# A two-layer decoder trunk: gated linear attention staggered against the projections around it

## The chip, the cores and the metric

The program runs on one core of a Trainium2 chip. Its time is the device time of one execution in microseconds (us); lower is better. The engines are TensorE (PE: matrix products and transposes, with the weight loads listed as PEld), VectorE (DVE), ScalarE (ACT), GpSimd (POOL) and SyncE (SP, which issues most loads). PE's products accumulate in eight PSUM banks of 512 float32 columns each.

## The reference, cut to what matters

Two layers work on 512 tokens of 1024 channels. Each layer normalizes, projects with one wide input matrix, runs three mixers side by side, adds their output projection, and then runs a feed-forward block. The change touches one mixer, the gated linear attention (4 heads, key width 32, value width 64), and the places of two projections around it:

```python
def reference(x, ...):
    for l in range(DEPTH):                                   # 2
        h = rmsnorm(x, attn_norm[l])
        (q, kc, vc, ksl, vsl, kwn, vwn, gts, gq, gk, gv, ga, gr, uv) = split_columns(h @ w_in[l])
        o_nsa = nsa_mixer(q, kc, vc, ksl, vsl, kwn, vwn, gts, ...)
        o_gla = gla_mixer(gq, gk, gv, ga, gr, gla_w_up[l], gla_b_up[l], gla_norm[l])
        o_sg = spatial_gating(uv, ...)
        x = x + jnp.concatenate([o_nsa, o_gla, o_sg], axis=-1) @ w_out[l]
        h = rmsnorm(x, ffn_norm[l])
        x = x + (jax.nn.silu(h @ w_gate[l]) * (h @ w_up[l])) @ w_down[l]
    return rmsnorm(x, final_norm)

def gla_mixer(q, k, v, a_lr, r, w_up, b_up, norm_g):
    g = log_sigmoid(a_lr @ w_up + b_up) / 16                 # (S, 4 heads, 32)
    ...
    def step(state, inp):                                    # one chunk of tokens
        bcum = jnp.cumsum(gc, axis=2)
        o_inter = jnp.einsum('bhck,bhkv->bhcv', qc * jnp.exp(bcum), state)
        decay = exp(where(causal, bcum[i] - bcum[j], -inf))  # per key channel
        attn = jnp.einsum('bhik,bhjk,bhijk->bhij', qc, kc, decay)
        o_intra = jnp.einsum('bhij,bhjv->bhiv', attn, vc)
        state = exp(blast) * state + einsum(kc * exp(blast - bcum), vc)
        return state, o_inter + o_intra
    ...
    return rmsnorm(o, norm_g) * silu(r)
```

## The kernel before, in words

**Projections.** The tokens are four tiles of 128. Every float32 operand of a projection is split into a high and a low part, and `mm3` (L327 to L329) makes one product out of three: high by high, high by low, low by high. `w_rows` (L315) loads a block of weights from SP's queue into a `raw` buffer (three of them); `w_split` (L305) makes the high part on ACT (L309) and the low part on DVE (L312) in an `hl` buffer (four of them). `proj_tok` multiplies a token tile at a time: 8 blocks of 128 channels by three products are 24 matmuls for a tile and 96 for a projection. The projections that matter here are gr (the gate r, 256 columns), B (keys and values of two branches of the sparse attention, 512 columns) and q (512 columns); `ev_gr`, `ev_b` and `ev_q` evacuate a tile's bank. `c1` is a small projection ahead of them, whose evacuation `ev_c1` also transposes a little tile `ga`.

**PSUM.** `psum(tag)` hands out banks by turns: g is banks 0 and 1 (projections), t is 2 and 3, s is 4 to 6, o is 7. The linear attention also names its banks directly.

**The linear attention.** The chunk of this kernel is a token tile, 128 wide, so there are four steps t = 0 to 3 with a state carried between them. A causal 128x128 block is cut into the diagonal and seven levels (squares of side 64, 32, ... 1), so that each square's decay splits into a factor for its queries and one for its keys. One step is a chain over engines:

1. Logits (L814, L815): a 0/1 matrix `tsel` times the split log gates gives sums of log gates for nine sets of 128 columns. They go through bank 6 in three groups of 512, 512 and 128 columns, and ACT takes each group's exp into `E` (L816).
2. Factors on DVE: seven products with the queries (L824, tile `xq`), two multiplies of `E` by the keys (L825, called xk in the code), and a fill of the diagonal of `at` by `diag` (L828).
3. Level products on PE (L834): 7 levels by 4 heads, 32 rows and 64 columns each, into banks 2 to 5.
4. Picks on DVE (L841): seven masked copies of the banks into `at`.
5. Outputs into bank 7: from the second step on, `xi` (queries by decay, on DVE) times the carried state `sbd`, a 128x256 matrix that is zero outside its four head blocks (L846), and `at` times the values for each head (L848). ACT copies the bank to `osb`.
6. Carry, not in the last step: a transpose of decayed keys (L853), a copy on ACT, the product with all values, 128x256 (L857), in bank 6, and on DVE the mask `bdm` and the update of `sbd` (L859, or L862 and L863).

**The order.** In the program's text gr stands before the four steps and B behind them. Engines run their own queues in order, but the order in each queue is made by a tile scheduler from the text and priorities: splits of weights are moved forward by 400 (`WPRI`), evacuations by 600 (`EPRI`). So in the queues as built, gr's matmuls stand ahead of the chain, and B's are laced through it. `tsel` is loaded at the start of a layer's mixer from ACT's queue into float32 and rounded by POOL to the type that PE wants (L791, L793). `diag` comes from the product of queries and keys, `qk`, made on POOL (L795) and summed by PE over each head (L798). Behind B come the key preparation `prep_k` (its transposes are L915), then q, then the sparse attention.

## Time and profile before

| what | value |
|---|---|
| median of 3 runs | 1318.18 us (1316.72 to 1322.44) |
| the profiled execution | 1317.21 us, of which the span 1315.4 us |
| PE busy | 97% of the span |
| DVE busy | 72% |
| ACT busy | 50% |
| POOL busy | 13% |
| DMA | 150.48 MB, 114 GB/s over the span |

The profile is one execution. Its span runs from the first to the last instruction, and the rows below give times in us from the span's start. A busy PE is not PE at its peak: the chip grants TensorE a clock that has two levels, 2.4 and 1.2 GHz, listed as a share (1.00 and 0.50), and a matmul is counted busy at either. The linear attention of layer 0 lies at about 94 to 160 us, that of layer 1 at about 737 to 806 us.

### The profile page before, as it was taken

What the parts mean: (1) busy time and instruction counts of PE and PEld (TensorE: products, weight loads), DVE (VectorE), ACT (ScalarE), POOL (GpSimd) and SP (SyncE); (2) the same over time, 40 slices, a digit from 0 to 9 for tenths busy, and PEclk for the clock granted to TensorE, in tenths of its full rate; (3) what the DMA queues carried; (4) which work ended last, traced back from release to release, by engine and by line L of the source; (5) the groups of instructions that cost most, each with busy time, mean ns of one, the idle gap of its engine ahead of it and who ended that gap; (6) DMA issues with size and microseconds to landing.
All of it is one profiled execution on the core that took longest, in us unless ns stands there. A gap on an engine that the chain in (4) does not pass through costs nothing.

```text
span 1315.4 us, 17968 instructions
## 1 busy us (share of the span) xinstructions
PE 1278.4 (97%) x6688; PEld 1045.4 (79%) x6688; DVE 944.5 (72%) x1637; ACT 658.5 (50%) x1200; POOL 174.0 (13%) x156
## 2 busy tenths in 40 slices
PE   8899999999999999999999999999999999999997
PEld 6788777778888888888888877677888888888786
DVE  5756889977855675577646578999777458736775
ACT  6663347865532543354446523678644435515532
POOL 2111121113000100010302102111210001000102
PEclk9998999999999999999999989999999999999999
DMA  7551221015334885483346302200533448754731
GB/s 234 143 162 40 65 64 33 17 64 145 96 101 123 208 229 141 108 200 107 110 104 168 105 9 64 81 17 17 137 103 96 114 129 211 219 128 127 195 96 64
DMA packets 128298, 150.48 MB, mean 114 GB/s; under 512 B 8778, under 2 KB 82260, under 8 KB 128212
## 3 DMA queue, kind: packets, MB, share of 16 engines
q1 hardware_dynamic: 116752, 129.07, 32.7%
q0 software_dynamic: 8704, 16.78, 7.6%
q10 hardware_dynamic: 2756, 3.50, 1.0%
q8 instruction: 52, 0.85, 0.3%
q14 instruction: 34, 0.28, 0.1%
HBM read 147.23 MB, written 2.10 MB: 114 GB/s over the span
## 4 chain that ended last, share of the span: by engine, by line
PE 74%; DVE 9%; ACT 3%; DMA 3%; issue 1%; POOL 0%; SPq 0%; ACTq 0%; DVEq 0%
PE banks L328 20%; PE banks L329 20%; PE banks L327 20%; PE banks L1082 2%; DVE hl L312 2%; PE banks L1095 2%; PE banks L1096 2%; DMA raw<-in_w_down_dram 1%; ACT hl L309 1%; PE banks L1057 1%; DVE P L1076 1%; PE banks L1058 1%; PE banks L834 1%; DMA wx<-in_w_up_dram 1%; PE banks L1039 1%
## 5 line engine op out<-in xcount | busy, mean ns | idle before, releaser
L309 ACT CAST hl<-raw 128x1024 fp32r<-128x1024 f32 (+3 forms) x186 | 192.2, 1036 | 234.5 <-PE banks L329 189.1
L312 DVE TENSOR_TENSOR hl<-raw,hl 128x1024 fp32r<-128x1024 f32 (+3 forms) x186 | 226.2, 1220 | 105.6 <-ACT hl L309 104.1
L327 PE MATMUL banks<-hl,kt 128*128 128x512 f32 (+2 forms) x696 | 262.5, 378 | 3.8 <-DVE act L292 1.6
L329 PE MATMUL banks<-hl,kt 128*128 128x512 f32 (+2 forms) x696 | 262.0, 377 | 0.0
L328 PE MATMUL banks<-hl,kt 128*128 128x512 f32 (+2 forms) x696 | 261.2, 376 | 0.5 <-DVE hl L312 0.5
L327 PEld LDWEIGHTS banks<-hl,kt 128*128 128x128 f32 x696 | 131.9, 190 | 28.2 <-DVE act L292 2.5
L327 PE MATMUL banks<-kt,hl 128*128 128x512 f32 x384 | 151.8, 397 | 2.3 <-DVE tmp L936 1.8
L328 PE MATMUL banks<-kt,hl 128*128 128x512 f32 x384 | 152.3, 397 | 0.0
L329 PE MATMUL banks<-kt,hl 128*128 128x512 f32 x384 | 152.0, 398 | 0.0
L328 PEld LDWEIGHTS banks<-hl,kt 128*128 128x128 f32 x696 | 131.9, 190 | 22.7 <-DVE hl L312 1.0
L329 PEld LDWEIGHTS banks<-hl,kt 128*128 128x128 f32 x696 | 131.9, 190 | 22.4 <-DVE kt L421 0.2
L309 ACT CAST hl<-wx 128x1024 fp32r<-128x1024 f32 x48 | 50.5, 1052 | 77.8 <-PE banks L329 70.3
L327 PEld LDWEIGHTS banks<-kt,hl 128*128 128x128 f32 x384 | 72.2, 188 | 16.5 <-DVE tmp L936 2.5
L328 PEld LDWEIGHTS banks<-kt,hl 128*128 128x128 f32 x384 | 72.5, 189 | 13.2 <-DVE kt L292 0.4
L329 PEld LDWEIGHTS banks<-kt,hl 128*128 128x128 f32 x384 | 72.4, 189 | 13.1
L312 DVE TENSOR_TENSOR hl<-wx,hl 128x1024 fp32r<-128x1024 f32 x48 | 58.7, 1223 | 18.5 <-ACT hl L309 18.3
L328 PE MATMUL banks<-act,hl 128*128 128x512 f32 x176 | 68.6, 390 | 0.6 <-DVE act L292 0.6
L329 PE MATMUL banks<-act,hl 128*128 128x512 f32 x176 | 68.5, 389 | 0.0
L327 PE MATMUL banks<-act,hl 128*128 128x512 f32 x176 | 68.2, 390 | 0.0
L438 DVE TENSOR_TENSOR xT<-xT,banks 128x512 f32<-128x512 f32 x56 | 37.4, 682 | 42.2 <-PE banks L329 42.1
L292 DVE TENSOR_TENSOR PT<-banks,PT 128x384 fp32r<-128x384 f32 (+1 forms) x96 | 54.7, 596 | 11.5 <-ACT PT L291 11.0
L327 PE MATMUL banks<-hl,act 128*128 128x512 f32 x160 | 62.5, 391 | 0.0
(347 smaller groups left out, 2408.3 us busy)
## 6 DMA issues: line engine op xcount, KB each, us to landing
raw<-in_w_gate_dram SPq DMA_DIRECT2D x44, 512.0 KB, 3.9
raw<-in_w_up_dram SPq DMA_DIRECT2D x44, 512.0 KB, 4.1
raw<-in_w_in_dram SPq DMA_DIRECT2D x32, 512.0 KB, 3.7
raw<-in_w_down_dram SPq DMA_DIRECT2D x20, 512.0 KB, 4.0
raw<-in_w_down_dram SPq DMA_DIRECT2D x36, 256.0 KB, 3.6
raw<-in_w_out_dram SPq DMA_DIRECT2D x16, 512.0 KB, 4.1
raw<-in_cmp_w_k_dram SPq DMA_DIRECT2D x8, 512.0 KB, 5.4
raw<-in_cmp_w_v_dram SPq DMA_DIRECT2D x8, 512.0 KB, 4.0
```

What stands on the lines that cost most here:

```text
L292: nc.vector.tensor_tensor(lo, src, hi.bitcast(F32), op=ALU.subtract)
L309: nc.scalar.copy(hl[:, 0, 0:n], raw[:, 0:n])
L312: e_.tensor_tensor(hl[:, 1, 0:n], raw[:, 0:n], hl[:, 0, 0:n].bitcast(F32), op=ALU.subtract)
L327: nc.tensor.matmul(ps, lh, rh, start=start, stop=False, skip_group_check=skip)
L328: nc.tensor.matmul(ps, lh, rl, start=False, stop=False, skip_group_check=skip)
L329: nc.tensor.matmul(ps, ll, rh, start=False, stop=stop, skip_group_check=skip)
L438: nc.vector.tensor_tensor(xT[:, m, :], xT[:, m, :], ps, op=ALU.add)
L834: nc.tensor.matmul(banks[:, 2 + h, lv * 64 : lv * 64 + 64], xk[r, lv, :], xq[r, lv, :], start=True, stop=True)
L1039: nc.tensor.matmul(S3, qs, kst[g][:, s_, :, 0:n], start=s_ == 0, stop=False)
L1082: nc.tensor.transpose(T[:, c : c + P], ps_[i][:, j * P : (j + 1) * P], ident)
L1095: nc.tensor.matmul(O[:, j * P : SEQ], lhs, pt[:, 0, c : c + n], start=first, stop=False)
L1096: nc.tensor.matmul(O[:, j * P : SEQ], lhs, pt[:, 1, c : c + n], start=False, stop=False)
```

## The change

The text of the linear attention is cut into `logits`, `factors`, `levels`, `pick`, `outputs` and `carry`, and the steps are staggered: the logits of step t+1 are written behind the levels of step t, and the factors of step t+1 behind its picks. Between them two tiles of a projection are written: gr in steps 0 and 1, B in steps 2 and 3 (`proj_one`, the body of `proj_tok` for one tile). The three groups of logits take banks 6, 7, 6. The outputs go into the level banks 2 to 5, 64 columns for each head. The state is 128x64 instead of 128x256: each head owns 32 rows, and both its product with the queries and its update are four products instead of one, of 32 rows and of 32 output partitions. The mask `bdm` is not used. `tsel` comes by one DMA from POOL's queue that converts as it writes, and `qk` is made on DVE. The transposes of `ga` in `c1` are written one tile later.

```diff
-                    nc.tensor.transpose(gps[0:17, t * P : (t + 1) * P], ga, ident)
+                    gas[t] = ga
...
+                proj_tok(c1_units(), 296, ev_c1, between=lambda t: turn_ga(t - 1) if t else None)
+                turn_ga(NT - 1)
...
-                site("gr")
-                proj_tok(units(C_GR, 256, (4, 4)), 256, ev_gr)
-
-                tself = gp.tile([P, 9 * P], F32, tag="E", name=nm("tself"), bufs=2)
-                nc.scalar.dma_start(tself, a["tsel"])
+                us_gr = units(C_GR, 256, (4, 4))
+                us_b = []
+
+                qk = tmp()
+                nc.vector.tensor_tensor(qk, qkT[0], qkT[1], op=ALU.mult)
                 tsel = gp.tile([P, 9 * P], F32R, name=nm("tsel"))
-                nc.gpsimd.tensor_scalar(tsel, tself, 1.0, None, op0=ALU.mult)
-                qk = tmp()
-                nc.gpsimd.tensor_tensor(qk, qkT[0], qkT[1], op=ALU.mult)
+                nc.gpsimd.dma_start(tsel, a["tsel"])
...
-                sbd = gp.tile([P, 256], F32, name=nm("sbd"))
+                state = gp.tile([P, DV], F32, name=nm("state"))
...
+                def logits(t):
+                    E = Es[t] = gp.tile([P, 9, P], F32, tag="E", name=nm("E"), bufs=2)
+                    for n, (c0, c1) in enumerate(((0, 4), (4, 8), (8, 9))):
+                        ps = banks[:, 6 + n % 2, 0 : (c1 - c0) * P]
+                        nc.tensor.matmul(ps, ghl[:, 0, tks(t)], tsel[:, c0 * P : c1 * P], start=True, stop=False)
+                        nc.tensor.matmul(ps, ghl[:, 1, tks(t)], tsel[:, c0 * P : c1 * P], start=False, stop=True)
                         nc.scalar.activation(E[:, c0:c1, :].rearrange("p l i -> p (l i)"), ps, AF.Exp, scale=1.0 / 16)
...
+                def outputs(t):
+
+                    E, at = Es[t], ats[t % 2]
+                    if t:
                         xi = tmp(P)
-                        nc.vector.tensor_tensor(xi, E[:, 8, :], qkT[0][:, tk], op=ALU.mult)
-                        nc.tensor.matmul(ops, xi, sbd, start=True, stop=False)
+                        nc.vector.tensor_tensor(xi, E[:, 8, :], qkT[0][:, tks(t)], op=ALU.mult)
+                        for h in range(GH):
+                            r = slice(DK * h, DK * h + DK)
+                            nc.tensor.matmul(banks[:, 2 + h, 0:DV], xi[r], state[r], start=True, stop=False)
                     for h in range(GH):
-                        nc.tensor.matmul(ops[:, h * DV : (h + 1) * DV], at[:, h, :], gv[:, t, h * DV : (h + 1) * DV],
-                                         start=t == 0, stop=t == 0 or h == GH - 1)
-                    nc.scalar.copy(osb[:, t, :], ops)
+                        nc.tensor.matmul(banks[:, 2 + h, 0:DV], at[:, h, :], gv[:, t, h * DV : (h + 1) * DV], start=t == 0, stop=True)
+                    nc.scalar.copy(osb[:, t, :].rearrange("p (h d) -> p h d", h=GH), banks[:, 2 : 2 + GH, 0:DV])
+
+                def carry(t):
+
+                    E = Es[t]
+                    kps = banks[:, 7, 0:P]
+                    nc.tensor.transpose(kps, E[:, 7, :], ident)
+                    ktok = tmp(P)
+                    nc.scalar.copy(ktok, kps)
+                    sps = banks[:, 7, 0:DV]
+                    for h in range(GH):
+                        r = slice(DK * h, DK * h + DK)
+                        nc.tensor.matmul(sps[r], ktok[:, r], gv[:, t, h * DV : (h + 1) * DV], start=True, stop=True)
+                    if t == 0:
+                        nc.vector.tensor_copy(state, sps)
                     else:
+                        nc.vector.scalar_tensor_tensor(state, state, E[:, 8, 127:128], sps, op0=ALU.mult, op1=ALU.add)
+
+                logits(0)
+                factors(0)
+                for t in range(NT):
+                    levels(t)
                     if t < NT - 1:
+                        logits(t + 1)
+
+                    if t == 1:
+                        us_b.extend(units(C_KS, 512, (2, 2, 2, 2)))
+                    for n in range(2):
+                        c = 2 * (t % 2) + n
+                        if t < 2:
+                            proj_one(c, us_gr, 256, ev_gr)
                         else:
+                            proj_one(c, us_b, 512, ev_b)
+                    pick(t)
+                    if t < NT - 1:
+                        factors(t + 1)
+                    outputs(t)
+                    if t < NT - 1:
+                        carry(t)
...
-            site("B")
-            proj_tok(units(C_KS, 512, (2, 2, 2, 2)), 512, ev_b)
```

In the changed kernel the lines are: logits L859 and L860, their exp L861; factors L871, L872 and L874; level products L882; picks L893; `xi` L900; outputs L903 and L905; carry L912 (transpose), L918 (products), L920 and L922 (state); the product qk L835; `diag` L840; the first transpose of `prep_k` L968.

How the queues change: SP's is the same instruction for instruction. On PE, DVE and ACT everything outside the two linear attentions stands in the same order, apart from the transposes of `ga`. In layer 0 the logits of steps 0 and 1 both stand near the start of gr: two groups of step 0 ahead of gr's first matmul, then 7 of gr's matmuls and `diag`, then the third group and the first two of step 1. Three places in detail:

PE, layer 0, between one step's outputs and the next step's levels (`at` by `gv` are the outputs, `tsel` by `ghl` logits, `xq` by `E` levels, `kt` by `hl` the projection that stands between). Before:

```order
L814 MATMUL banks<-tsel_1071,ghl_874 128x512
L815 MATMUL banks<-tsel_1071,ghl_874 128x512
L848 MATMUL banks<-gv_247,at_1083 128x64 x4
L329 MATMUL banks<-hl_1402,kt_99 128x512
L814 MATMUL banks<-tsel_1071,ghl_874 128x128
L815 MATMUL banks<-tsel_1071,ghl_874 128x128
L834 MATMUL banks<-xq_1163,E_1153 128x64 x28
L846 MATMUL banks<-sbd_1082,tmp_1209 128x256
L853 MATMUL banks<-ident,E_1153 128x128
L327 MATMUL banks<-hl_1402,kt_99 128x512
```

After:

```order
L328 MATMUL banks<-hl_947,kt_99 128x256
L329 MATMUL banks<-hl_947,kt_99 128x256
L905 MATMUL banks<-gv_247,at_962 128x64 x4
L912 MATMUL banks<-ident,E_966 128x128
L859 MATMUL banks<-tsel_952,ghl_874 128x512
L860 MATMUL banks<-tsel_952,ghl_874 128x512
L327 MATMUL banks<-hl_942,kt_96 128x256
L328 MATMUL banks<-hl_942,kt_96 128x256
L882 MATMUL banks<-xq_1092,E_1015 128x64
L918 MATMUL banks<-gv_247,tmp_1109 32x64 x4
L882 MATMUL banks<-xq_1092,E_1015 128x64 x27
```

Before, the three groups of logits of a step stand one by one between matmuls of B, the levels follow the last of them at once, and the transpose of the carry stands behind the levels. After, the outputs of step 0 stand behind the last matmul of a gr tile and the transpose right behind them; the levels are those of step 1, whose logits were made a step before, and the logits that follow are those of the step after. The carry's four products stand inside the levels.

DVE, layer 0, the first picks of step 0 (copies of the banks into `at`) and what is ahead of them. Before:

```order
L828 COPY_PREDICATED at_1085<-m_75,diag_1079 128x512
L825 TENSOR_TENSOR E_1087<-E_1087,gqk_878 128x512
L841 COPY_PREDICATED at_1083<-m_75,banks 128x256
L841 COPY_PREDICATED at_1083<-m_75,banks 128x128x2
L841 COPY_PREDICATED at_1083<-m_75,banks 128x64x4
L859 TENSOR_TENSOR sbd_1082<-banks,cf 128x256
L841 COPY_PREDICATED at_1083<-m_75,banks 128x32x8
L841 COPY_PREDICATED at_1083<-m_75,banks 128x16x16
L841 COPY_PREDICATED at_1083<-m_75,banks 128x8x32
```

After:

```order
L871 TENSOR_TENSOR xq_1092<-gqk_877,E_1015 128x64 x5
L872 TENSOR_TENSOR E_1015<-E_1015,gqk_878 128x512
L871 TENSOR_TENSOR xq_1092<-gqk_877,E_1015 128x64 x2
L874 COPY_PREDICATED at_964<-m_75,diag_958 128x512
L872 TENSOR_TENSOR E_1015<-E_1015,gqk_878 128x512
L893 COPY_PREDICATED at_962<-m_75,banks 128x256
L893 COPY_PREDICATED at_962<-m_75,banks 128x128x2
L893 COPY_PREDICATED at_962<-m_75,banks 128x64x4
```

Before, what stands just ahead of the first pick is the end of the factors, the fill of another `at` and a multiply of another `E`: step 1's. After, all of step 1's factors stand there: seven products into `xq`, two multiplies of `E` and the fill.

DVE, layer 0, the last pick of step 3 (`at`, 128x4x64) and its neighbours at the end of B (`vst` and `tmp` from the banks and `rstd` are `ev_b`, `hl` from `raw` the split of a weight of q). Before:

```order
L841 COPY_PREDICATED at_1085<-m_75,banks 128x32x8
L841 COPY_PREDICATED at_1085<-m_75,banks 128x16x16
L841 COPY_PREDICATED at_1085<-m_75,banks 128x8x32
L841 COPY_PREDICATED at_1085<-m_75,banks 128x4x64
L883 SCALAR_TENSOR_TENSOR vst_243<-banks,rstd_237,vst_243 128x2x64 x2
L891 SCALAR_TENSOR_TENSOR tmp_1507<-banks,rstd_237,cf 128x128
L893 SCALAR_TENSOR_TENSOR tmp_1508<-banks,rstd_237,cf 128x2x32
```

After:

```order
L811 SCALAR_TENSOR_TENSOR tmp_1513<-banks,rstd_237,cf 128x128
L813 SCALAR_TENSOR_TENSOR tmp_1514<-banks,rstd_237,cf 128x2x32
L816 SCALAR_TENSOR_TENSOR tmp_1514<-banks,rstd_237,cf 128x2x32
L312 TENSOR_TENSOR hl_1619<-raw_1617,hl_1619 128x1024
L893 COPY_PREDICATED at_964<-m_75,banks 128x4x64
L900 TENSOR_TENSOR tmp_1529<-E_1299,gqk_877 128x128
L964 COPY tmp_1570<-kr_939 128x512
```

Before, the last pick stands ahead of an evacuation of B. After, it stands behind the last evacuation of B and behind the split of q's fourth weight, and the product for the last step's state (`tmp` from `E`) stands behind it; the copies for `prep_k` follow.

## Rows read from the trace of the kernel before

**Rows 1.** The page's first part: busy time, share of the span, instructions of each engine

```profile
PE 1278.4 (97%) x6688; PEld 1045.4 (79%) x6688; DVE 944.5 (72%) x1637; ACT 658.5 (50%) x1200; POOL 174.0 (13%) x156
```

**Rows 2.** Stretches: length, busy time (instructions) by engine, PE's granted clock, DMA

```profile
105.00:120.00 15.00, 15.00 (x104) 11.73 (x103) 9.74 (x18) 4.32 (x8) 2.58 (x3) 0.77 0.25 72
...
775.00:795.00 20.00, 18.49 (x120) 13.80 (x120) 13.56 (x42) 3.90 (x11) 1.83 (x2) 0.83 0.01 1
```

**Rows 3.** PE by time, layer 0: start, duration, line, operation, count, idle time before

```profile
94.49 0.38 PE L327 MATMUL banks<-hl,kt 128*128 128x256 f32 x1
...
105.98 0.28 PE L329 MATMUL banks<-hl,kt 128*128 128x256 f32 x1
...
107.25 1.05 PE L798 MATMUL banks<-cf,tmp 128*128 128x4 f32 x8
```

**Rows 4.** PE by time: one step of the chain in layer 0

```profile
126.69 0.50 PE L814 MATMUL banks<-tsel,ghl 128*128 128x512 f32 x1
...
128.67 0.39 PE L327 MATMUL banks<-hl,kt 128*128 128x512 f32 x1
...
129.36 0.39 PE L327 MATMUL banks<-hl,kt 128*128 128x512 f32 x1
129.59 1.00 PE L848 MATMUL banks<-gv,at 128*128 128x64 f32 x8
...
130.65 0.44 PE L328 MATMUL banks<-hl,kt 128*128 128x512 f32 x1
131.02 1.85 PE L834 MATMUL banks<-xq,E 32*128 32x64 f32 x56
132.81 0.70 PE L846 MATMUL banks<-sbd,tmp 128*128 128x256 f32 x2
...
133.97 0.70 PE L857 MATMUL banks<-gv,tmp 128*128 128x256 f32 x2
...
135.28 0.50 PE L814 MATMUL banks<-tsel,ghl 128*128 128x512 f32 x1
```

**Rows 5.** PE by time: the same stretch in layer 1

```profile
737.60 0.39 PE L327 MATMUL banks<-hl,kt 128*128 128x256 f32 x1 [0.81 <-DVE gqk L772]
...
777.52 0.40 PE L815 MATMUL banks<-tsel,ghl 128*128 128x512 f32 x1
778.60 0.50 PE L814 MATMUL banks<-tsel,ghl 128*128 128x512 f32 x1 [0.69 <-ACT E L816]
```

**Rows 6.** The chain that ended last: start, length, what; where `prep_k` begins

```profile
160.67 1.15 PE banks L915 x8
...
805.87 1.14 PE banks L915 x8
```

**Rows 7.** DVE by time: factors of one step, and seven picks

```profile
128.94 0.79 DVE L824 TENSOR_TENSOR xq<-gqk,E 128x64 f32<-128x64 f32 x5
129.65 0.68 DVE L825 TENSOR_TENSOR E<-E,gqk 128x512 f32<-128x512 f32 x1
...
130.62 0.73 DVE L828 COPY_PREDICATED at<-m,diag 128x512 f32<-128x512 uint8 x1
...
143.94 3.86 DVE L841 COPY_PREDICATED at<-m,banks 128x256 f32<-128x256 uint8 x7
```

**Rows 8.** ACT by time: the first exp of layer 0

```profile
95.86 0.60 ACT L816 ACTIVATE E<-banks 128x512 f32<-128x512 f32 x1
```

**Rows 9.** The page: the split on DVE (mean ns), and loads (us to landing)

```profile
L312 DVE TENSOR_TENSOR hl<-raw,hl 128x1024 fp32r<-128x1024 f32 (+3 forms) x186 | 226.2, 1220 | 105.6 <-ACT hl L309 104.1
...
raw<-in_w_in_dram SPq DMA_DIRECT2D x32, 512.0 KB, 3.7
...
wx<-in_w_up_dram POOLq DMA_DIRECT2D x8, 512.0 KB, 9.0
```

**Rows 10.** The tile `tsel`: engine, operation, ns min/median/max, first and last start

```profile
L793 POOL TENSOR_SCALAR tsel<-tself x2: 3134/3136/3137, 75.7 to 719.6; 128x1152 fp32r<-128x1152 f32 x2
```

**Rows 11.** DVE by time: an evacuation of q in layer 0

```profile
173.29 0.75 DVE L931 SCALAR_TENSOR_TENSOR qr<-banks,rq,cf 128x512 f32<-128x512 f32 x1 [1.89 <-PE banks L329]
```

107 lines of the change are left out of this document (53 added, 54 removed).

## The prediction

> **What bounds the kernel now.** I read the page's busy line first [rows 1]: PE is busy for 97% of the span and DVE for 72%. A chain that waits can therefore save time only where PE's queue stands behind it, or where a busy PE does little: at the lower clock, or between matmuls of different shape. So the second view is the stretches around the two linear attentions [rows 2]. PE looks full there, yet the granted clock averages 0.77 over 15 us in layer 0 and 0.83 over 20 us in layer 1. The clock has two levels, 2.4 and 1.2 GHz, so 0.23 x 15 = 3.4 us and 0.17 x 20 = 3.4 us of clock are missing. In both layers the fall follows a thin piece of PE's queue: the short products of levels and of `diag` in layer 0 [rows 3], and in layer 1 two waits of PE on one bank [rows 5].
>
> The third view is PE in order of time. I sum over the stretch from the first gr matmul to the first transpose of `prep_k`: 94.49 to 160.67, 66.2 us, and 737.60 to 805.87, 68.3 us [rows 3, 5, 6]. Its contents are the same in both layers, and apart from the small fp32 products the same in both kernels:
> - gr, 96 matmuls 256 wide: 95 steps in 105.98 - 94.49, so 0.121 each, 11.6 us [rows 3];
> - 96 of B and 26 of q, 512 wide: three steps in 129.36 - 128.67, so 0.23 each, 28.1 us [rows 4];
> - four steps of the chain. A clean one lasts 135.28 - 126.69 = 8.6 us [rows 4] and holds 14 matmuls of B (3.2), so the chain's own part is 5.4 with its changes of shape. Four of them, the last without carry (0.6 less, since L857 alone takes 0.70 [rows 4]): 21.0;
> - `diag`, 1.0 [rows 3].
>
> Together 61.7 us. Layer 0 is over that by 4.5, or by 5.0 since its first pair of logits (2 x 0.23) stands ahead of the stretch: 3.4 of clock and 1.6 of waits. Layer 1 is over by 6.6: 3.4 of clock, 1.7 for two waits on bank 6 (1.08 between L815 and the next L814 instead of 0.23, twice [rows 5]), 1.5 of other waits.
>
> **The change part by part.**
> *Logits in banks 6 and 7, one step ahead.* This takes away layer 1's 1.7 us, since the second group no longer waits until the exp has read the first, and exp and factors run under projection work. One such wait remains at the start of layer 0: logits of two steps come before any real cover. The exps start at 95.86 and take 0.60 each [rows 8]; the third, short one ends near 97.35. PE gets there at 94.7 + 7 gr matmuls (0.85) + 0.2 for the product qk, now on DVE + `diag` 1.05 [rows 3], about 96.8. It waits 0.6, with the 0.2 makes 0.8. Layer 1 has gr matmuls between those groups: 0.
>
> *gr in steps 0 and 1, B in steps 2 and 3.* No matmul, DMA or split is added; SP issues the same loads in the same order. What is late next is the pick of step 0. DVE has factors(1) ahead of pick(0) in its queue: products at 0.79 for five of the seven, two multiplies of E at 0.68 and one `at` fill at 0.73, each starting a little before the one ahead has ended, some 2.9 us; then the seven picks, 3.86 [rows 7]. I put the end of factors(0) at 99.8, so pick(0) ends near 106.6. PE ends levels(0) at 101.2 and has 35 gr matmuls left (4.2): 105.4. So outputs(0) make PE wait 1.2 us; in layer 1, by the same walk, 1.0. In steps 1 to 3 PE has 43 to 46 matmuls between levels and outputs (5.5 us of gr, 10 of B) against some 4.9 of DVE: no wait.
>
> *Outputs per head into the level banks, state in row groups.* Removed per step: L846 and L857, 256 wide. Added: four products of 32 rows (L903) and four of 32 columns (L918), 8 records each. At the pitch of the level products (131.02 to 132.81 for 56, 0.032) 8 records cost 0.26; at that of the old outputs (1.00 for 8) up to 1.0 [rows 4]. None of the rows shows a 32-column product. A change into the 32-row shape costs 0.37 - 0.23 = 0.14 (130.65 to 131.02) [rows 4], and a step has three to four more of them. Three carries per layer: between -0.8 (all at 0.26, the old pair gone) and +3 us (1.0 each and 0.14 per change). I take +0.4, near the level products, whose form L903 shares. The Trainium skill, "TensorEngine Tiling (Array Packing)", section Tiling Modes, says that changing the tiling mode drains the engine; the 0.14 us agrees that a change costs something, and by that rule alone, at 0.14 for some 11 extra changes, the term would be +1.5 per layer and the forecast 2 us later. DVE's state update shrinks from 256 to 64 columns; it runs beside PE, so I count nothing, and if that cover were gone it could only gain.
>
> *Casting DMA for `tsel`.* The cast on POOL is done at 75.7 + 3.1 = 78.8 and 722.7 [rows 10], 15 us before the first gr matmul. A transfer from POOL's queue lands in up to 9.0 us [rows 9] after an issue that stands behind the same memset; it stays hidden. Cost 0; it would have to land 15 us late to count.
>
> *c1's transposes one tile later.* PE's gaps there are below what the rows resolve: 0.
>
> *q's weights behind the last picks.* The last two picks and the product for outputs(3) now stand on DVE among q's four splits. Splits take 1.22, a load 3.7 [rows 9], and the fourth load needs the buffer that the first split frees. I get the product done 5.8 us after B ends, and PE reaches outputs(3) after 26 matmuls of q, 6.0 us. So 0.3 us for q's fourth weight, no more.
>
> *The sum.* Layer 0 after: 61.7 - 0.9 (two pairs ahead of the stretch) + 0.2 (the second pair's tail) + 0.8 + 1.2 + 0.4 + 0.3 = 63.7, against 66.2: 2.5 less. Layer 1: 61.7 - 0.5 + 1.0 + 0.4 + 0.3 = 62.9 against 68.3: 5.4 less. Together 7.9. The profiled execution took 1317.21 us for a span of 1315.4, so 1309.3; the median of the three runs is 1.0 higher than that execution, so 1310.3. What follows keeps it: in q DVE has idle time of 1.89 before one evacuation [rows 11], more than the 1.2 us of picks that move there.
>
> **The rivals.**
> *The low clock stays.* The wait for pick(0), followed by outputs and level products, is again a thin piece of PE's queue, 2 to 5 us long; so is layer 0's start. For it: the falls of before came after just such pieces. Against it: the clean steps, with the same products but B in between, fell nowhere. One fall costs 3.4: 1313.7; one per layer 1317.1.
>
> *The gain is not passed on.* If DVE is late at the end of B, the start of attention waits on q's evacuations as it does now, and what PE saved stands idle there: 1315 to 1318. Against it the idle 1.89 us.
>
> *Slower.* Outputs(3) stand in PE's queue ahead of 70 matmuls of q. Their last pick is behind the fourth split on DVE, which waits for a load, which waits for the first split. Every microsecond beyond 0.2 that this chain is late is one of PE, in each layer. It eats the gain at about 4 us per layer (a load landing in 8 instead of 3.7), and gives 1325 or more at 11 us instead of 3.7. For it: DVE is the engine behind there. Against it: the same four splits follow B now, and loads land in 3.7 at the median.
>
> *More than forecast.* If the carry costs -0.8 and the walk's waits are gone: 3 us per layer more, 1304.
>
> **How the numbers follow.** Forecast without a fall of the clock 0.47 (own range 1306 to 1313.5); the low clock stays once 0.28, twice 0.09; not passed on 0.06; slower 0.06; more 0.04. The range, 1303 to 1320, adds a microsecond or two at its ends for the spread of the runs shown (1316.72 to 1322.44) and leaves out the slower case. A difference of 0.5%, 6.6 us, is about what a measurement of this kernel can tell from none; the line is 1311.6. Under it lie about three quarters of the forecast (0.36), a quarter of the one-fall case (0.07) and the best case: 0.47. Over 1324.8 lies the slower case: 0.06. Within: 0.47.
>
> **What would show it.** Right: no stretch at a lower clock in either linear attention; no L860 with a gap of 1.08 behind it; about 1.2 us of PE idle before the first L905 of each layer, released by DVE's pick; first L968 2 to 6 us earlier after the first gr matmul, three q matmuls more counted in. The carry term is read from the pitch of L903 and L918. Wrong: a granted clock below 1 around step 0; PE idle before the last L903 of a layer; an exp waiting for `tsel`; or q's end earlier and attention's first scores not.

## The result, and the profile after

| | median | range | runs |
|---|---|---|---|
| before | 1321.51 us | 1316.72 to 1326.0 | 7 |
| changed | 1312.74 us | 1309.35 to 1315.21 | 7 |

The ratio is 0.9933, 95% interval 0.9909 to 0.9956: 8.8 us less, where the prediction had 7.9 less and 1310.3 us. The 1310.3 was counted from the median of three runs of before, 1318.18; the seven here have 1321.51, so it is the difference that agrees. It is made of other terms than those forecast, as the views below show. The profiled execution of the changed kernel took 1313.64 us for a span of 1311.9; its pair of before is the 1317.21 us ahead.

The page's busy line of the changed kernel answers to [rows 1]:

```profile
PE 1274.4 (97%) x6760; PEld 1046.3 (80%) x6760; DVE 942.4 (72%) x1635; ACT 658.5 (50%) x1200; POOL 168.7 (13%) x154
```

PE is as full as before, so the time came out of what PE does and at which clock, not out of idle time that the page counts. The same view as [rows 2], the changed kernel (length, busy time of PE, PEld, DVE, ACT and POOL with their instructions, granted clock, DMA share, GB/s):

```profile
95.00:160.00 65.00, 64.02 (x578) 54.33 (x578) 50.66 (x134) 23.35 (x46) 10.12 (x9) 1.00 0.19 58
745.00:765.00 20.00, 18.43 (x170) 17.02 (x169) 14.18 (x33) 6.85 (x15) 2.88 (x4) 0.83 0.02 3
```

In layer 0 the clock stays at 2.4 GHz through the whole linear attention. In layer 1 there is still a stretch at 1.2: 0.17 x 20 = 3.4 us of clock are missing, as before, but now around step 0. The two places where PE waits for the picks of step 0, which answer to [rows 3, 5], in PE by time (start, duration, line, tiles, idle time before and who ended it):

```profile
105.72 0.28 PE L329 MATMUL banks<-hl,kt 128*128 128x256 f32 x1
106.80 1.10 PE L905 MATMUL banks<-gv,at 128*128 128x64 f32 x8 [0.80 <-DVE at L893]
```

```profile
748.21 0.28 PE L329 MATMUL banks<-hl,kt 128*128 128x256 f32 x1
750.06 1.10 PE L905 MATMUL banks<-gv,at 128*128 128x64 f32 x8 [1.57 <-DVE at L893]
751.09 0.32 PE L918 MATMUL banks<-gv,tmp 128*32 128x64 f32 x8
751.34 0.33 PE L859 MATMUL banks<-tsel,ghl 128*128 128x128 f32 x1
751.51 0.27 PE L860 MATMUL banks<-tsel,ghl 128*128 128x128 f32 x1
751.71 2.55 PE L882 MATMUL banks<-xq,E 32*128 32x64 f32 x56
754.19 0.80 PE L859 MATMUL banks<-tsel,ghl 128*128 128x512 f32 x1
```

After the longer wait the clock falls at 752.5, in the middle of the level products: these take 2.55 instead of the 1.79 of layer 0 at full clock, and the next logits 0.80 instead of 0.50. And the piece that answers to [rows 4], outputs and carry of step 1 in layer 0:

```profile
118.31 0.39 PE L329 MATMUL banks<-hl,kt 128*128 128x512 f32 x1
118.63 0.45 PE L903 MATMUL banks<-state,tmp 32*128 32x64 f32 x8
119.01 1.10 PE L905 MATMUL banks<-gv,at 128*128 128x64 f32 x8
120.05 0.32 PE L918 MATMUL banks<-gv,tmp 128*32 128x64 f32 x8
120.29 0.50 PE L327 MATMUL banks<-hl,kt 128*128 128x512 f32 x1
```

From start to start, the state's product takes 0.38 (118.63 to 119.01), the outputs 1.04 (119.01 to 120.05) and the update 0.25 (120.05 to 120.29). What follows L848, L846 and L857 in the step of before at [rows 4]:

```profile
130.39 0.30 PE L814 MATMUL banks<-tsel,ghl 128*128 128x128 f32 x1
...
133.34 0.27 PE L853 MATMUL banks<-ident,E 128*128 128x128 f32 x1
...
134.32 0.58 PE L328 MATMUL banks<-hl,kt 128*128 128x512 f32 x1
```

So before the outputs take 0.80 (from 129.59), the state's product 0.53 (from 132.81) and the update 0.35 (from 133.97). The three together are 1.67 after and 1.68 before: what the narrow products save is lost again at the outputs, which now stand between them.

**How stretches are compared.** Totals of one kernel spread by 6 us and more. So each profile is cut at landmarks that all kernels share: E, from the first matmul behind the key compression to the last matmul of gqk (the projection ahead of the logits); and S, from the last matmul of gqk to the last of q (96 matmuls each of gr, B and q lie in it). The start times come from PE in order of time. Half the time spent at half clock is taken off S and given beside it; it is the most that a fall can cost, and less where PE waits inside it. E is given as it was measured. "S at equal content" in two of the expectations ends at the first transpose of `prep_k`, less 0.23 for each matmul of q over 26.

| kernel | S layer 0 (clock) | S layer 1 (clock) | E layer 0, 1 |
|---|---|---|---|
| before | 81.8 (3.4) | 83.7 (3.4) | 33.0, 32.9 |
| before, second profile | 82.5 (0) | 83.7 (3.4) | 33.0, 32.9 |
| changed | 79.5 (0) | 79.7 (3.4) | 33.9, 33.6 |
| changed, second profile | 79.6 (0) | 79.8 (1.7) | 33.8, 36.4 |
| logits of step 1 later | 78.6 (0) | 78.6 (0) | 34.1, 36.3 |
| gr first | 80.2 (1.7) | 80.0 (0) | 33.9, 33.6 |
| one bank | 80.3 (0) | 80.4 (3.4) | 33.6, 36.3 |
| wide state | 81.8 (0) | 82.4 (3.4) | 33.8, 38.2 |
| old `tsel` | 79.6 (0) | 79.6 (3.4) | 32.7, 33.3 |
| longer wait | 79.3 (0) | 80.1 (3.4) | 37.2, 36.2 |
| before, two banks | 83.2 (0) | 84.2 (0) | 32.9, 32.9 |
| later logits, old `tsel` | 78.6 (0) | 78.5 (0) | 32.7, 33.3 |
| later logits, late cast | 78.6 (0) | 78.5 (0) | 32.7, 33.4 |
| before, narrow state | 84.4 (8.5) | 84.9 (8.5) | 32.9, 33.0 |

The change takes 2.3 and 4.0 us of work and waits out of S (3.0 in layer 0 against the second profile of before), and gives 0.9 and 0.7 or more back in E.

Where the 3.0 are: the second profile of before and the first of the changed kernel have no fall in S of layer 0, and their PE records can be summed by kind, from start to start without idle time. The level products take 7.2 instead of 8.4, the 287 projection matmuls up to the last one of q 57.1 instead of 58.3, the logits 5.6 instead of 5.8; state's product, outputs and update together 5.8 instead of 5.9; idle time is 1.0 instead of 1.2, and small pieces make 0.2. So the three products with the state make little of the difference. Most of it is the same work with fewer breaks: before, the level products of step 0 come in pieces of 10, 22 and 24 records with `diag` and matmuls of B between them (the 22 take 0.06 each, where 0.03 is the pace of the other steps), and B is broken up more often by pieces of the chain.

### The profile page after: what moved, and what is told of

Its sections match the earlier page's. It is cut to its first block, busy times and chain, and to the rows that moved or that the text cites. A ratio compares the mean times of both kernels' runs of the same rounds, so it can differ in the third digit from the quotient of the medians.

```text
span 1311.9 us, 18107 instructions
## 1 busy us (share of the span) xinstructions
PE 1274.4 (97%) x6760; PEld 1046.3 (80%) x6760; DVE 942.4 (72%) x1635; ACT 658.5 (50%) x1200; POOL 168.7 (13%) x154
## 4 chain that ended last, share of the span: by engine, by line
PE 73%; DVE 6%; DMA 3%; ACT 2%; issue 1%; POOL 0%; SPq 0%; ACTq 0%; DVEq 0%; POOLq 0%
PE banks L327 20%; PE banks L328 20%; PE banks L329 20%; PE banks L1135 3%; PE banks L1148 2%; PE banks L1149 2%; DMA raw<-in_w_down_dram 1%; PE banks L1110 1%; DVE P L1129 1%; ACT hl L309 1%; PE banks L1111 1%; DVE hl L312 1%; PE banks L1441 1%; DMA wx<-in_w_up_dram 1%; PE banks L1092 1%
## 5 line engine op out<-in xcount | busy, mean ns | idle before, releaser
L327 PE MATMUL banks<-hl,act 128*128 128x512 f32 x160 | 62.5, 391 | 0.0
```

The lines of the kernel that those rows point to most:

```text
L327: nc.tensor.matmul(ps, lh, rh, start=start, stop=False, skip_group_check=skip)
```

## The experiments

**The changed kernel again** (no edit).

> The changed kernel once more, unchanged, for a second profile. From the last matmul of the projection before (gqk) to the first transpose of prep_k, at equal content (26 matmuls of q), the first profile of the changed kernel has 62.0 us in layer 0 without a fall of the clock and 65.6 in layer 1 with one fall of 6.83 us at half clock at 752.5; before has 67.6 and 69.5, with one fall in each. Theory A, a fall belongs to its place in the program (a thin piece of PE's queue after the wait for the pick of step 0): the same fall near 752 and none in layer 0, so 62.0 and 65.6 again. Theory B, a fall hits or spares such a place by how the execution lies against the chip's clock control: the falls stand elsewhere than in the first profile; a stretch without one is 62 in either layer, one with is 65 to 66. Ratio to before 0.991 to 0.996 by both.

Measured: 1310.85 us, ratio 0.9939 (0.9918 to 0.9959). At equal content 62.1 in layer 0 without a fall and 64.0 in layer 1 with one of 3.41 us at 756.3. Theory A holds for the place: the fall is again in layer 1, right behind the wait for the picks of step 0 (1.6), and not in layer 0 (0.8). Theory B holds for the size, 3.41 us instead of 6.83, and for falls elsewhere: this profile has one at 712.0 that the first lacks.

**Logits of step 1 later.**

```diff
-                    if t < NT - 1:
+                    if 0 < t < NT - 1:
                         logits(t + 1)
...
                             proj_one(c, us_gr, 256, ev_gr)
                         else:
                             proj_one(c, us_b, 512, ev_b)
+                        if t == 0 and n == 0:
+                            logits(1)
```

> The logits of step 1 are written behind the first gr tile of step 0 instead of ahead of it, so that the picks of step 0 no longer stand behind all factors of step 1 on DVE. Theory A, PE's idle time ahead of the first outputs (0.96 us in layer 0, 1.73 in layer 1) is made by factors(1) ahead of pick(0) on DVE: it goes to under 0.3 in layer 0 and falls below 1 in layer 1, the stretch from gqk to prep_k at equal content is 61.0 to 61.7 in layer 0, and layer 1 has no fall of the clock and comes to 61.5 to 62.5. Rival, the wait only moves: PE stands idle ahead of levels(0) instead (nothing else is there to cover factors(0) but gr), and the stretch stays at 62 or grows to 63. The total is within 0.3% of the changed kernel by both.

Measured: 1309.12 us, ratio 0.9930 (0.9904 to 0.9956); at equal content 61.1 and 61.0. The wait in layer 0 in PE by time, and in layer 1 the stretch that was at half clock (columns as above):

```profile
107.08 1.10 PE L905 MATMUL banks<-gv,at 128*128 128x64 f32 x8 [0.28 <-DVE at L893]
```

```profile
745.00:765.00 20.00, 20.00 (x287) 17.70 (x288) 18.51 (x48) 8.34 (x18) 3.11 (x4) 1.00 0.14 39
```

Theory A holds: the wait was made by the factors of step 1 ahead of the picks of step 0. It is 0.28 in layer 0 and none in layer 1; the fall of the clock is gone with it, and S is 1.0 shorter in both layers. In the total the step is inside the intervals.

**gr first.**

```diff
+                for c in range(NT):
+                    proj_one(c, us_gr, 256, ev_gr)
...
-                    for n in range(2):
-                        c = 2 * (t % 2) + n
-                        if t < 2:
-                            proj_one(c, us_gr, 256, ev_gr)
-                        else:
-                            proj_one(c, us_b, 512, ev_b)
+                    proj_one(t, us_b, 512, ev_b)
```

> The changed kernel with all of gr written ahead of the steps, as before, and one tile of B written in each step. Theory A, what the change gains is the missing thin piece (levels, diag and bank waits that before follow each other without projection work between) and the shorter steps, wherever the cover comes from: with 24 matmuls of B in each step (5.5 us) the steps stay covered, and the stretch at equal content is 61.5 to 63.5 in both layers. Rival, gr between the steps is what covers the start: without it PE waits ahead of the outputs of each step for DVE, 0.5 to 1.5 us per step, and the stretch goes back to 65 to 68, most of the gain.

Measured: 1316.08 us, ratio 0.9974 (0.9960 to 0.9988). At equal content 64.2 with a fall of 3.41 us (so 62.5 without) and 62.3; S is 0.3 to 0.7 longer than in the changed kernel. Theory A holds for the stretch: where the cover comes from matters little. The total is 0.35% worse than that of the changed kernel in the same comparison, more than the stretches explain; the mean granted clock (0.9928 against 0.9936 over ten runs each) is 1.0 us of it. The profiled execution, at 1312.8, is among the fastest of its ten, and where the others lose the rest is open.

**One bank for the logits.**

```diff
-                        ps = banks[:, 6 + n % 2, 0 : (c1 - c0) * P]
+                        ps = banks[:, 6, 0 : (c1 - c0) * P]
```

> The changed kernel with all three groups of logits in bank 6. Theory A, the second bank matters where two groups follow each other with nothing between: PE waits about 0.85 us for an exp there, which the trace of before shows twice in layer 1; the scheduler has projection matmuls to put between in all steps but at the start of each layer, so the stretch grows by 0 to 1 us per layer. Rival, the second bank carries the gain: four steps with one or two waits of 0.85 each, 3.4 to 6.8 us more per layer. A fall of the clock adds 3.4 by either.

Measured: 1314.12 us, ratio 0.9967 (0.9945 to 0.9990); S 0.5 to 0.7 longer in each layer. Theory A: with the logits a step ahead the second bank is worth that much a layer.

**Wide state.**

```diff
-                            r = slice(DK * h, DK * h + DK)
-                            nc.tensor.matmul(banks[:, 2 + h, 0:DV], xi[r], state[r], start=True, stop=False)
+                            nc.tensor.matmul(banks[:, 2 + h, 0:DV], xi, state[:, h * DV : (h + 1) * DV], start=True, stop=False)
...
-                        nc.tensor.matmul(sps[r], ktok[:, r], gv[:, t, h * DV : (h + 1) * DV], start=True, stop=True)
+                    nc.tensor.matmul(sps, ktok, gv[:, t, :], start=True, stop=True)
```

> The changed kernel with the state as a 128x256 matrix again: its product with the queries is four products of all 128 rows instead of 32, its update one product of 128x256 instead of four of 32 columns, with the mask on DVE. Stretch = from the last matmul of gqk to the last matmul of q, less the clock that is missing in it: 79.5 us in layer 0 and 79.7 in layer 1 in the changed kernel, 81.8 and 83.7 before. In the trace of the changed kernel the four products of 32 rows (8 records) take 0.38 from start to start and the four of 32 columns 0.25. Theory A, the narrow forms are cheap and the changes of shape are in these pitches already: the wide forms cost 0.8 to 1.0 (at the pitch of the outputs) and 0.35, so each of three carries is 0.4 to 0.6 longer and the stretch 81 in both layers, 1.2 to 1.8 more. Rival, each change into a 32-row or 32-column form costs 0.14 or more somewhere else: without them the stretch is the same or up to 1 us shorter.

Measured: 1317.61 us, ratio 0.9991 (0.9972 to 1.0011): next to nothing of the gain is left. S is 81.8 and 82.4, so 2.3 and 2.8 longer. PE by time, the same place as in the changed kernel above:

```profile
118.75 1.10 PE L902 MATMUL banks<-state,tmp 128*128 128x64 f32 x8
119.69 1.06 PE L904 MATMUL banks<-gv,at 128*128 128x64 f32 x8
120.59 0.65 PE L915 MATMUL banks<-gv,tmp 128*128 128x256 f32 x2
120.89 0.58 PE L327 MATMUL banks<-hl,kt 128*128 128x512 f32 x1
```

The four products of all rows take 0.94 (0.84 in the later steps) where those of 32 rows take 0.38, and the outputs behind them 0.90 where they took 1.04. Theory A holds, above its size. PE's order is nearly that of the changed kernel, so the difference can be placed: behind the last outputs of the layer the wide form is 1.8 us (layer 0) and 2.2 us (layer 1, with 0.7 of waiting for a weight's split) later at the same count of projection matmuls, and the other 0.6 come at the key preparation, where PE waits 0.4 for DVE.

This wide form is not that of before. Before has one product of 256 columns with the state (0.53); outputs per head into four banks need four, and these are dearer. So the experiment prices the narrow state within the new order, not against before. Read with the kernel before with two banks (below), which has the same four wide products, the three parts form a ladder of S: outputs per head and two banks in the old order, 83.2 and 84.2; with the new order, 81.8 and 82.4; with the narrow state, 79.5 and 79.7.

The Trainium skill, "TensorEngine Tiling (Array Packing)", section Tiling Modes, has a change of tiling mode drain the engine; by that alone the wide form, with fewer changes, would be the faster one. The measurement decides against it here: the changes do cost something (the outputs take 1.04 between narrow products and 0.90 between wide ones), but less than the narrow products save.

**`tsel` as before.**

```diff
-                nc.gpsimd.dma_start(tsel, a["tsel"])
+                tself = gp.tile([P, 9 * P], F32, tag="E", name=nm("tself"), bufs=2)
+                nc.scalar.dma_start(tself, a["tsel"])
+                nc.gpsimd.tensor_scalar(tsel, tself, 1.0, None, op0=ALU.mult)
```

> The changed kernel with the 0/1 matrix as before: a load on ACT's queue into float32 and the rounding on POOL. PE's queue is the same. Theory A, either way it is there long before the first logits: the stretch from the last matmul of gqk to the last of q, less missing clock, is 79.5 and 79.7 again within 0.3, and the total that of the changed kernel within 0.3%. Rival, POOL's 3.1 us of rounding or the load in ACT's queue delay something in the stretch before (the memsets, the value compression): the first logits of a layer come 0.5 to 2 us later after the layer's beginning.

Measured: 1307.84 us, ratio 0.9915 (0.9885 to 0.9944). S is the same, 79.6 in both, but E is 32.7 instead of 33.9 in layer 0, and 33.3 in layer 1. Neither theory had that: the casting DMA costs, and not where its result is used. ACT and POOL by time; the changed kernel first, then the kernel with later logits and this old load, which has the same start of layer 0:

```profile
61.47 0.74 POOL L837 DMA_DIRECT2D tsel<-in_tsel_dram  x1
...
66.03 0.93 ACT L309 CAST hl<-raw 128x888 fp32r<-128x888 f32 x1 [2.19 <-DMA raw<-in_w_in_dram]
...
68.28 0.69 ACT L309 CAST hl<-raw 128x592 fp32r<-128x592 f32 x1 [0.72 <-DMA raw<-in_w_in_dram]
```

```profile
64.84 0.94 ACT L309 CAST hl<-raw 128x888 fp32r<-128x888 f32 x1 [1.61 <-DMA raw<-in_w_in_dram]
66.60 0.69 ACT L309 CAST hl<-raw 128x592 fp32r<-128x592 f32 x1 [0.22 <-DMA raw<-in_w_in_dram]
...
70.73 0.35 ACTq L838 DMA_DIRECT2D tself<-in_tsel_dram  x1
```

The casting DMA leaves POOL at 61.5, as soon as POOL is free, among the loads of c1's weights, and ACT waits 1.1 us longer for two of them (2.19 + 0.72 against 1.61 + 0.22). The old load stands in ACT's queue and so goes out 9 us later, behind those loads. In layer 1 the chain goes on to PE. POOL, ACT and PE by time in the second profile of the changed kernel:

```profile
703.95 0.61 POOL L837 DMA_DIRECT2D tsel<-in_tsel_dram  x1
...
709.95 0.93 ACT L309 CAST hl<-raw 128x888 fp32r<-128x888 f32 x1 [4.12 <-DMA raw<-in_w_in_dram]
...
710.93 0.40 PE L327 MATMUL banks<-hl,kt 128*128 128x296 f32 x1 [1.77 <-ACT hl L309]
```

The load is late, so is the split, PE waits 1.77 us for it, and the clock falls at 712.0. Five of the seven profiles with the early cast have such a wait of 1.6 to 2.0 at this place, and in the same five the clock falls 0.6 to 2 us behind it. In the other two the wait is 0.6 or none and no fall begins there, and no profile with the old load or the late cast has such a wait or fall.

**A longer wait.**

```diff
-                    nc.vector.copy_predicated(ats[t % 2], eye8..., diag...)
+                    for _ in range(3 if t == 1 else 1):
+                        nc.vector.copy_predicated(ats[t % 2], eye8..., diag...)
```

> The changed kernel with the fill of the diagonal for step 1 done three times instead of once on DVE, so that DVE is later at the picks of step 0 (or at those of step 1) by 1.4 us. Theory A, the fall of the clock in layer 1 follows the thin piece that begins with PE's wait for the picks of step 0, and a longer wait there brings it to layer 0 as well: a fall of 3.41 or 6.83 us within 10 us behind the first outputs in both layers, and the stretch from the last gqk to the last q matmul, less missing clock, 80.5 to 81.2 in both. Rival, the falls come by how the execution lies against the clock's control and not by the wait: none in layer 0 again, the same stretch without clock. If the two more fills land between picks and factors where DVE has time, the stretch stays at 79.5.

Measured: 1315.96 us, ratio 0.9965 (0.9943 to 0.9987), but the edit did not make the wait: 0.8 in layer 0 and 1.8 in layer 1, since the scheduler put the fills among the picks and moved the outputs. The fall is in layer 1 again, none in layer 0. It says nothing against theory A and does not test it. By the ratios the total is 3.4 us longer than that of the changed kernel; the mean granted clock of its ten runs is 0.9909 against 0.9936, which is 3.5 us. Why the clock falls more often was not found.

**Before with two banks.**

```diff
-                        ps = banks[:, 6, 0 : (c1 - c0) * P]
+                        ps = banks[:, 6 + n % 2, 0 : (c1 - c0) * P]
...
-                        nc.tensor.matmul(ops, xi, sbd, start=True, stop=False)
+                        for h in range(GH):
+                            nc.tensor.matmul(banks[:, 2 + h, 0:DV], xi, sbd[:, h * DV : (h + 1) * DV], start=True, stop=False)
...
-                        kps = banks[:, 6, 0:P]
+                        kps = banks[:, 7, 0:P]
```

> The kernel before with one part of the change: logits in banks 6 and 7, and for that the outputs per head in the level banks and the carry in bank 7; the order of the text, gr ahead of the steps, the wide state and tsel stay as before. Stretch from the last matmul of gqk to the last of q less missing clock: 81.8 in layer 0 and 83.7 in layer 1 before. Theory A, the two banks take away the two waits of 0.85 that layer 1 has, and little in layer 0, while the state's product in four pieces costs 0.3 to 0.5 in three steps: 82 to 83 in both layers, with a fall of the clock in each as before; so the rest of the gain (2.3 to 4 us per layer and the clock) comes from the stagger. Rival, the banks are the larger part: 80 in both layers.

Measured: 1315.85 us, ratio 0.9974 (0.9954 to 0.9995). S is 83.2 and 84.2, 0.7 to 1.4 and 0.5 longer than in the two profiles of before: the four wide products take 2.6 in three steps where the one of before takes 1.4, and that eats what the second bank saves in layer 1. No fall in either layer, which theory A did not expect. The rival falls.

**Later logits and old `tsel`; later logits and a late cast.** Both with the second experiment's edit; the second of them with

```diff
+                nc.gpsimd.tensor_scalar(tsel[:, 0:16], gv[:, 1, 0:16], 1.0, None, op0=ALU.mult)
                 nc.gpsimd.dma_start(tsel, a["tsel"])
```

> Both edits that helped together: logits of step 1 behind the first gr tile, and the 0/1 matrix by ACT's queue and POOL as before. Theory: they act in different places and add. Stretch from the last matmul of gqk to the last of q, less missing clock, 78.6 us in both layers (as with the logits moved), the last gqk matmul of layer 0 at 90.5 to 91.5 us less the clock missing before it (as with the old load; 93.6 and 94.0 in the two profiles of the changed kernel), no wait for the picks of step 0. Ratio to before 0.988 to 0.992. Rival, the entry differs by chance from execution to execution and not by the load: last gqk at 93 to 94 again, ratio 0.992 to 0.994.

> Logits of step 1 behind the first gr tile, and the casting DMA kept, but issued some 12 us later: POOL writes 16 columns of the matrix's tile from the values of the second token tile first, and the DMA behind that. Theory A, the casting DMA costs because it is issued at 61.5 us beside the loads of c1's weights, whose splits ACT then waits for (2.19 us for one load instead of 1.26): issued behind them it costs nothing, and the last gqk matmul of layer 0 stands at 90.5 to 91.5 less missing clock, as with the old load. Rival B, the kind of DMA or its queue costs whenever it runs: 93 to 94. Stretch from gqk to q 78.6 in both layers, if the matrix lands in time; if it lands late the first exp waits and the stretch grows by that.

Measured: 1305.28 us, ratio 0.9909 (0.9882 to 0.9936), and 1306.12 us, ratio 0.9901 (0.9877 to 0.9924), the two best medians of the study. S is 78.6 and 78.5 in both, and neither has a fall in the linear attention. The forecast place of the last gqk matmul, 90.5 to 91.5, was wrong (92.15 and 93.05, the second of them within what rival B had). It had taken the 1.7 us of a fall at 51 off the 92.3 of the old load, but with no fall ahead of it the matmul still stands at 92.15. By E, which is local, both stand at 32.7 in layer 0 as with the old load. POOL by time in the second:

```profile
75.66 0.78 POOL L838 DMA_DIRECT2D tsel<-in_tsel_dram  x1 [0.32 <-POOL tsel L837]
```

The same casting DMA 14 us later costs nothing that E shows (32.7 and 33.4, against 32.7 and 33.3 with the old load). So it is the time of issue, not the kind of DMA: theory A.

**Before with the narrow state.**

```diff
-                        nc.tensor.matmul(ops, xi, sbd, start=True, stop=False)
+                        for h in range(GH):
+                            r = slice(DK * h, DK * h + DK)
+                            nc.tensor.matmul(banks[:, 2 + h, 0:DV], xi[r], state[r], start=True, stop=False)
...
-                        nc.tensor.matmul(sps, ktok, gv[:, t, :], start=True, stop=True)
+                        for h in range(GH):
+                            r = slice(DK * h, DK * h + DK)
+                            nc.tensor.matmul(sps[r], ktok[:, r], gv[:, t, h * DV : (h + 1) * DV], start=True, stop=True)
```

> The kernel before with one part of the change: the state as 128x64 in row groups, its product with the queries four products of 32 rows, its update four of 32 columns, and for that the outputs per head in the level banks; logits in one bank, gr ahead, tsel as before. Theory A, per carry the pair costs 0.38 + 0.25 instead of 0.54 + 0.35 (starts to starts in the traces of the changed kernel and before): 0.26 less, three times, 0.8 per layer; the stretch from the last gqk matmul to the last of q, less missing clock, is 80.8 to 81.3 in layer 0 and 82.6 to 83.1 in layer 1 (81.8 and 83.7 before). Theory B, the narrow state is the larger part of the gain, as the wide state in the changed kernel (81.8 and 82.4) could be read: 79.5 to 80 in layer 0.

Measured: 1334.21 us, ratio 1.0125 (1.0097 to 1.0154), a surprise to both theories. PE by time in layer 0, and the two stretches around it:

```profile
133.21 0.32 PE L859 MATMUL banks<-gv,tmp 128*32 128x64 f32 x8
136.81 0.70 PE L847 MATMUL banks<-state,tmp 32*128 32x64 f32 x8 [3.27 <-DVE at L841]
137.44 1.97 PE L849 MATMUL banks<-gv,at 128*128 128x64 f32 x8
139.17 0.77 PE L814 MATMUL banks<-tsel,ghl 128*128 128x512 f32 x1
139.74 0.63 PE L815 MATMUL banks<-tsel,ghl 128*128 128x512 f32 x1
141.10 0.80 PE L814 MATMUL banks<-tsel,ghl 128*128 128x512 f32 x1 [0.74 <-ACT E L816]
```

```profile
130.00:155.00 25.00, 20.30 (x181) 15.90 (x180) 14.59 (x44) 3.14 (x9) 1.46 (x2) 0.66 0.00 1
782.00:807.00 25.00, 19.47 (x177) 15.24 (x177) 14.97 (x44) 3.04 (x8) 1.46 (x2) 0.66 0.01 2
```

With the narrow state the scheduler laid the matmuls of B differently and left none for the step from 2 to 3. PE waits 3.27 for the picks, then runs outputs, logits and levels one behind the other, and the clock stays low: (1 - 0.66) x 25 = 8.5 us in each layer. The narrow products themselves are as short as in the changed kernel. It is a loss of the kind that the prediction's slower rival feared, in another place: the products that serve the staggered order go with a loss where nothing stands between the links of the chain.

**Before again** (no edit).

> The kernel before once more, unchanged, for a second profile. Its first profile has falls of the clock at 51.1 (3.41 us), 109.1 and 781.5 (6.83 us each). Theory A, the two falls in the linear attention belong to their place, the thin pieces there: falls within 5 us of 109 and 781 again, and the stretch from the last gqk matmul to the last q matmul 84 to 86 and 86 to 88. Theory B, they come by how the execution lies against the chip's clock control: one or both are missing, the stretch without is 81.8 in layer 0 or 83.7 in layer 1 and the falls stand elsewhere. The stretch from the first product behind the key compression to the last gqk matmul, 32.9 in both layers by either.

Measured: 1316.59 us beside 1315.81, one run each. S is 82.5 without a fall in layer 0, and 83.7 with one of 6.83 us at 779.9 in layer 1. The stretch at [rows 2] for layer 0 again, now at full clock:

```profile
105.00:120.00 15.00, 14.69 (x147) 11.67 (x145) 12.68 (x28) 5.32 (x11) 2.32 (x3) 1.00 0.25 72
```

So the fall in layer 1 comes each time, the one in layer 0 does not.

## Why the prediction was right, and where it was wrong

The time and the direction were right. Of its terms:

- **The clock.** Forecast: 3.4 back in each layer, with one fall left as the next likely case (1313.7). Measured: none in layer 0 in any profile of the changed order of steps with gr between, but before has it there only in one of two; in layer 1 a fall remains in both profiles, which by the prediction's own list is a sign of being wrong. So of 6.8 us, 0 to 5.1 came back, depending on which profiles are paired. Over all its runs the changed kernel has a mean clock of 0.9936 against 0.9921 of before in the comparison with its second profile, which is 0.0015 x 1311 = 2.0 us of the 7.6 between the means (1311.5 and 1319.2).
- **The wait for the picks of step 0** took the place of the bank's, as forecast: 0.8 instead of 1.2 in layer 0, 1.6 instead of 1.0 in layer 1, released by DVE. That it could pull the clock down was the rival. The five profiles with a wait of 1.5 to 1.8 there all have a fall in layer 1 within 3 us of its end, and the three in which that wait is gone have none. The kernel with one bank has its fall a step later, behind a wait of 0.6 for `xi`, so a short wait does not rule a fall out.
- **Bank 6.** Layer 1's two waits are gone, as forecast. The 0.6 forecast at the start of layer 0 did not come: the third group follows `diag` at once.
- **The carry was mis-sized.** Forecast +0.4 per layer, between -0.8 and +3. The narrow products alone are some 0.7 shorter than the old pair, near the lower bound, so the row of the level products was the right one for both forms. But the changes of shape show at the outputs between them: per step 0.38 + 1.04 + 0.25 against 0.53 + 0.80 + 0.35, no difference, and over the layer -0.1. (The 1.00 that the prediction took from the old outputs is a duration; from start to start they take 0.80.)
- **The steps.** The prediction kept the chain's own part of a clean step at 5.4. A whole step, from one transpose of the carry to the next, is 133.24 - 117.26 = 15.98 with 48 matmuls of B (11.0 at 0.23), so 4.9 for the chain, against 8.59 - 14 x 0.23 = 5.4 in the clean step of before: 0.4 less, 1.3 over three steps, for which the sum has no term.
- **The casting DMA was forecast at 0 and is the step that failed.** The prediction asked whether the matrix is there in time, and it is. It did not ask what the transfer meets at its new time of issue, 61.5 instead of 71.4 us. It costs 1.2 us of E in layer 0 against the old load, and in layer 1 E is 33.6 to 34.8 without the missing clock, against 33.3; in five of seven profiles with the early cast a fall of the clock also begins inside E (at 68, and at 710 to 716), in none of the seven with the old load or the late cast. (The 9.0 us to landing that the prediction read as a bound is a median [rows 9]; this transfer landed in 5.8.)
- **q's last weight** forecast at 0.3: PE does not wait there. In layer 0 that nearly closes the account: work and waits were to grow by 0.9 (2.5 less with 3.4 of clock) and fell by 2.3, and of the 3.2 between, the steps are 1.3, the start 0.6, the carry's 0.4, the picks 0.4 and this weight 0.3.
- **Passed on.** The rival by which the gain is lost again behind q falls: from the last matmul of q in layer 0 to the start of E in layer 1 it is 525.2 and 524.9 us before and 525.1 and 525.3 after, less missing clock.

So the sum was right by terms that cancelled, and that the total came so close is luck. The clock was forecast at 6.8 and gave 2.0 on average; work and waits in S were forecast at 7.9 - 6.8 = 1.1 and gave 2.3 + 4.0 = 6.3, by steps and level products with fewer breaks and, in layer 1, by the waits for bank 6; E was forecast unchanged and took 0.9 + 0.7 = 1.6, nearly all of it the early cast (1.2 and 0.3 against the old load). Together 6.7, where the means of the runs have 7.6. The profiled pair shows only 3.57 of the 9.7 by which the two stretches S are shorter with their clock: 1.6 went at E, and 4.9 behind the two stretches, where the changed kernel has three falls of the clock (at 237, 698 and 882 us, 1.7 each) and before none. The fall of before at 51 gave back 0.4 only: PE's next wait, at 57.7, is 0.84 with it and 1.86 in the second profile of before without it.

The experiments point to a version that beats both kernels: the logits of step 1 later and `tsel` out of the way of c1's loads, 1305 to 1306 us, 0.9 to 1.0% under before. Against the changed kernel the intervals of the totals overlap; there it is the stretches that show the gain, 1.0 in each S and 1.2 and 0.3 in E.

## What to carry to other kernels

A transfer that is early enough for its user may still be too early for its neighbours: look at which loads are in flight when the queue that issues it falls free. A saving of work on an engine that is 97% busy pays only where other work fills the gap behind it; the same narrow products took 2.3 and 2.8 us off the stretch of a layer in the staggered order, and went with a loss of some 17 in all, most of it clock, where the scheduler left a hole. A control that puts one part back must put back its old form: four wide products are not the one wide product of before. And when totals spread by half a percent, cut the traces at landmarks that both kernels share, and count missing clock apart.

## What was not expected of the hardware

Four products of 32 rows took 0.38 and four of 32 columns 0.25, where four with all rows and as many columns took 0.84 to 0.94; one product of 256 columns took 0.30 to 0.53. The outputs between the narrow ones took 1.04 instead of 0.80 to 0.90. One wait of PE for 1.5 to 1.8 us ahead of outputs and level products was followed by 1.2 GHz in layer 1 in five profiles of five, a wait of 0.8 at the same place in layer 0 in none; 3.27 us followed by a bare chain held it low for 8.5 us' worth of clock. The length of the wait alone does not decide: PE waits 1.75 us at 57.3 in the first profile of the changed kernel too, and no fall follows there.
